# An RWKV-7 scan on one core: a substitution moved from VectorE to GpSimd, a multiply-add for the state, and another scheduler

## The chip, the cores and the metric

The kernel runs on one core of a Trainium2 chip. The metric is the device time of one execution in microseconds (us), the median of several runs of the same program. A profile is taken of one further execution; its span runs from the first to the last instruction.

Engines are named as in the profile: PE is TensorE (matrix products; PEld its weight loads), DVE is VectorE, ACT is ScalarE, POOL is GpSimd, SP is SyncE, which issues the DMAs here. Each engine works through a queue of its own in a fixed order; an instruction that waits for a semaphore holds up all behind it in that queue. SBUF is the on-chip memory, PSUM the banks that PE writes.

## The reference, cut to what matters

One encoder layer: x (1024 positions, 1024 channels) is normalised and multiplied by one wide matrix w_in; three mixers (an mLSTM, a long convolution by FFT, a bidirectional RWKV-7) work on parts of the product; their outputs are gated, merged, projected and added to x. The change is in the third mixer and in the scheduling of everything.

```python
def rwkv7_scan(r, w, k, v, kk, a, reverse):
    def step(state, inp):
        r_t, w_t, k_t, v_t, kk_t, a_t = inp
        sa = jnp.einsum('bhij,bhj->bhi', state, -kk_t)
        state = (state * w_t[:, :, None, :] + sa[..., None] * (kk_t * a_t)[:, :, None, :]
                 + v_t[..., None] * k_t[:, :, None, :])
        return state, jnp.einsum('bhij,bhj->bhi', state, r_t)
...
    y_fwd = rwkv7_scan(r_h, dec_h[:, :, 0], k_dir[:, :, 0], v_h, kk, a_h[:, :, 0], reverse=False)
    y_bwd = rwkv7_scan(r_h, dec_h[:, :, 1], k_dir[:, :, 1], v_h, kk, a_h[:, :, 1], reverse=True)
```

There are 16 heads of 64 channels, two directions and 1024 positions.

## The kernel before

**Chunks.** The scan works on pairs of heads (8 pairs) and chunks of 64 positions (16 chunks, `CL = 64`): 8 x 16 = 128 steps, each for two heads and both directions (d = 0 forward, d = 1 backward) at once. Inside a chunk the delta rule is a triangular system. Its inverse, the table `tt`, is computed ahead of the scan for eight chunks, both directions and both heads together, which I call a substitution: `tphase(cx, g)`, g = 0 for steps 0 to 7 and g = 1 for steps 8 to 15 of a pair, 16 substitutions in all.

**A substitution** (`tphase`, L1597): block products on PE (tile pq), copied by ACT to `quad` and `q21`; a transpose on DVE into `Ab`; a loop of 31 rounds l, each a multiply into `tm` of 31-l by l//2+1 elements per partition and an add into `Tb`, through the helper `self.tt` (L476, DVE); two more transposes on DVE (t1, t2); two rounds of small products on PE (tile pwx) with copies by ACT (W, tt). Each round needs the one before it.

**A step of the scan** (`scan`, L1740, one turn of the loop over m): U = products of G and SV on PE (tile pch); copied by DVE to `us`; SA = products of tt and us; copied into SV by DVE (first head) and ACT (second head); SN = products of B and SV; the state S1 = (SN + S0) x pc on DVE, two operations (pc is the decay of the chunk); S1 copied into the next step's SV, one half by DVE, one by ACT. Then the next step's U can start. The outputs of a step, products [G, SV] and [ar, sn], are issued inside the next step (`outputs`, `late`). `in_turn` (L391) issues a group of products one behind the other, with the lines L395 (first) and L398 (the rest).

**Other work of a pair**: `prep` (decays and scaled keys, on ACT and DVE; two-operand DVE work on tiles s, P, a, tmp, ar, bk; its small tile `s` is cleared by a POOL memset), `setup` (G, B and SV of the next two steps: products pgr and ptv), `load`, `bonus`, `post`.

**Fillers.** All products with w_in and later the branch projections are jobs (`gemm`, L343: 512-column products into tile pg, three for each weight: L351 to L353). Ahead of the scan they fill the other mixers; inside it `weave` (L72) lets a step yield four times and takes a share of the jobs that are left at each (`fill`). A weight tile is loaded by SP (`wraw`, 3 buffers), rounded by ACT (`wh`) and its remainder is made by POOL (`wl<-wraw,wh`, L334, 4 buffers).

**What sets the order.** The program is written with a tile framework: a list scheduler orders each engine's queue from the traced program, by priority; `high_priority(n)` moves instructions ahead by n, `issue_after` keeps one behind another on an engine. `put(gen, steps...)` in `rwkv` says at which yields of a pair (64 of them, 4 per step) a generator of other work is advanced.

Of the kernel before, what the change touches and what calls it, by code (L numbers as in the profile page):

```python
# [11 lines left out]
F32 = mybir.dt.float32  # L12
F32R = mybir.dt.float32r
AF = mybir.ActivationFunctionType
# [9 lines left out]
TP, PP, PW, RA = 400, 0, 3, 2  # L24
NP, ND = 3, 2
SA, SB = 100, 16
TAIL = (21, 22, 23)
CDEC = math.exp(-0.5)
MUL, ADD, SUB, MAX, MIN = ALU.mult, ALU.add, ALU.subtract, ALU.max, ALU.min
# [30 lines left out]
def ahead(tc, gen, by):  # L60

    while True:
        if by:
            with tc.high_priority(by):
                if next(gen, gen) is gen:
                    return
        elif next(gen, gen) is gen:
                return
        yield
# [43 lines left out]
class Row0:  # L113
# [133 lines left out]
    def first(self, w1t, bf):  # L247

        acc = self.ts(w1t[:, 0:1], 0.0, MUL)
        for i in range(1, 17):  # L250
            acc = self.tt(acc, w1t[:, i:i + 1], ADD)
        return self.act(acc, bf, 0)
# [33 lines left out]
class Trunk:  # L286
# [104 lines left out]
    def in_turn(self, calls, ins=None):  # L391

        for f in calls:
            if ins is None:
                ins = f()  # L395
                continue
            with self.tc.issue_after(ins.ins), self.tc.high_priority(10 ** 6):
                ins = f()  # L398
        return ins

    def banks(self, name):

# [944 lines left out]
    def rwkv(self, yc_out, pairs=range(8)):  # L1347
        nc, tc, A = self.nc, self.tc, self.A
        with ExitStack() as c2:
# [37 lines left out]

            pairs = list(pairs)
            n = len(pairs)
            cx = [dict(p=p, ar={}, al={}, bk={}, pc={}) for p in pairs]  # L1390
            run(self.load(cx[0]))
            for g in range(2):
# [8 lines left out]
            for i in range(n):  # L1401
                at = {}

                def put(gen, *steps):
                    for s in steps:
                        at.setdefault(s, []).append(gen)
                put(prep1, 0, 0, 1, 2, 3, 4, 4)
                put(self.bonus(cx[i]), 5, 6, 7)
                put(ahead(tc, self.tphase(cx[i], 1), TP), *range(6, 28, 2))
                if i + 1 < n:  # L1410
                    nx = cx[i + 1]
                    put(self.load(nx, cx[i - 1] if i else None), 8, 9, 10, 11)
                    put(ahead(tc, self.prep(nx, 0, 0), PP), 15, 16, 19, 33, 33)
                    put(ahead(tc, self.prep(nx, 0, 1), PP), 34, 35, 36, 37, 37)
                    put(ahead(tc, self.tphase(nx, 0), TP), *range(39, 62, 2))
                    prep1 = ahead(tc, chain(self.prep(nx, 1, 0), self.prep(nx, 1, 1)), PP)
                    put(prep1, 40, 42, 49)
                if i > 0:
                    put(self.post(cx[i - 1], yc_out, i + 1 == n), 5, 6, 7, 8, 11, 12, 13, 14)
                weave(self.scan(cx[i], cx[i + 1] if i + 1 < n else None), at, self.fill, max(0, self.left() - 6) / (64.0 * (n - i + 0.1)))  # L1420
# [176 lines left out]
    def tphase(self, cx, g):  # L1597

        nc, rp = self.nc, self.rp
        x2 = lambda n: self.ep.tile([128, 16, 32], F32, name=n, tag="x2", bufs=3)
        q, q21 = x2("quad"), self.ep.tile([128, 16, 32], F32, name="q21", tag="q21", bufs=1)
        pq = [x.rearrange("p (c t) -> p c t", t=CL) for x in self.banks("pq")]
# [25 lines left out]
        for l in range(31):  # L1630
            n, m = 31 - l, l // 2 + 1
            x = tm[:, 0:n * m].rearrange("p (a b) -> p a b", b=m)
            self.tt(x, Ab[:, l + 1:32, l].unsqueeze(2).broadcast_to([128, n, m]),
                    Tb[:, l, 0:m].unsqueeze(1).broadcast_to([128, n, m]))
            o = Tb[:, l + 1:32, 0:m]
            self.tt(o, o, x, ADD)
            if l % 5 == 4:
                yield
        tt = self.tt_t[g]
        t1 = x2("t1").rearrange("p a b -> p (a b)").rearrange("p (v s) -> p v s", s=16)  # L1640
        nc.vector.transpose(t1.rearrange("p v s -> p s v"), Tb.rearrange("p t s -> p s t"))
        t1 = t1.rearrange("p (g u) s -> p u s g", g=2)
        t2 = x2("t2")
        nc.vector.transpose(t2.rearrange("p u (s g) -> p u s g", g=2), t1)
# [95 lines left out]
    def scan(self, cx, nx):  # L1740
# [13 lines left out]
        for m in range(16):  # L1754
# [11 lines left out]
            if late:  # L1766
                late[0](ins)
            us = self.sm.tile([128, 2, CL], F32, name="us", tag="us", bufs=2)
            nc.vector.tensor_copy(us, U)  # L1769
            ins = self.in_turn(partial(nc.tensor.matmul, SA[hsl[h], d], tt[hsl[h], 8 * d + c, :], us[hsl[h], d],  # L1770
                                       start=True, stop=True) for d in range(2) for h in range(2))
            if late:
                late[1](ins)
            late = None
            nc.vector.tensor_copy(SV[0:64, 0, both], SA[0:64])
            nc.scalar.copy(SV[0:64, 1, both], SA[64:128])  # L1776
            yield
            next(ahead, None)
            yield
            self.in_turn(partial(nc.tensor.matmul, SN[hsl[h], d], B[:, j, d, hsl[h]], SV[:, h, at[d]],  # L1780
                                 start=True, stop=True) for d in range(2) for h in (1, 0))
            S1 = self.sm.tile([128, 2, 64], F32, name="sn", tag="sn", bufs=3)
            pc = cx["pc"][g][:, :, c:c + 1].broadcast_to([128, 2, 64])
            if m == 0:
                self.tt(S1, SN, pc)
            else:
                self.tt(S1, SN, S0, ADD)
                self.tt(S1, S1, pc)
            late = self.outputs(y, py, m, S0, ar, now)
            S0 = S1  # L1790
            if m < 15:
# [5 lines left out]
            if m < 15:  # L1797

                SV, at = now[2], now[4]
                nc.vector.tensor_copy(SV[0:64, 0, at], S1[0:64])  # L1800
                nc.scalar.copy(SV[0:64, 1, at], S1[64:128])  # L1801
            yield
            next(ahead, None)
            yield
# [111 lines left out]
```

## Time and profile before

| | |
|---|---|
| median of 3 runs | 2182.08 us (2180.28 to 2186.04) |
| profiled execution, its span | 2200.05 us, 2198.3 us |
| granted PE clock, mean | 0.956 |
| ahead of the scan, scan, behind it (first and last product of pch) | 929, 1059, 210 us |
| PE, DVE, ACT, POOL busy | 1994.0, 1634.6, 1103.2, 424.3 us |
| substitution loop (tm and Tb of L476), 16 x 62 operations on DVE | 145.4 + 144.2 us |
| POOL: wl split, 408 operations | 371.5 us |

A line of a group in the profile reads: line, engine, operation, output<-inputs by the program's names, shapes, count | busy us, mean ns of one | idle us of that engine just before them, and what ended it. A line of the timeline reads: start us, us, engine, line, operation, names, shapes, count, and in brackets the engine's idle time before it and who ended it.

### The profile page before, as it was taken

To read this page: it belongs to the slowest core of one execution; us is meant where nothing else is said; L and a number is where in the kernel's file an instruction comes from. 1 tells how busy PE (TensorE), PEld (TensorE's weight loads), DVE (VectorE), ACT (ScalarE), POOL (GpSimd) and SP (SyncE) were. 2 spreads that over 40 slices of the span, in tenths; PEclk is the share of its full clock that TensorE was granted. 3 is DMA by queue.
4 is the path that set the end of the run, shared out by engine and by line. 5 is a ranking of instruction groups with operands and counts; after the bars stand their busy time and mean duration, and the time that the engine had idled before them with its cause. 6 is when DMAs were issued, how large, how long until landed. Compare 5 with 4: busy or idle time off the path is not lost. (4 is left out here: it accounts for less than half of the span.)

```text
span 2198.3 us, 45984 instructions
## 1 busy us (share of the span) xinstructions
PE 1994.0 (91%) x17098; PEld 1509.2 (69%) x17098; DVE 1634.6 (74%) x4754; ACT 1103.2 (50%) x2558; POOL 424.3 (19%) x485
## 2 busy tenths in 40 slices
PE   6999899999989899899989999999898887897998
PEld 4666777787868677666766676666666665675786
DVE  4854999988447947788787888868887888764536
ACT  5557356454242115664665756667466564532221
POOL 2211311122222432311101111111114411010200
PEclk9999999999999999999998999999899998897999
DMA  8211222334465345321322333224143542445623
GB/s 255 70 67 59 78 77 90 112 101 127 143 200 172 119 138 163 124 68 61 130 79 93 117 106 102 92 81 136 52 155 118 187 144 63 159 143 175 196 89 129
DMA packets 169384, 262.19 MB, mean 119 GB/s; under 512 B 17863, under 2 KB 87335, under 8 KB 169160
## 3 DMA queue, kind: packets, MB, share of 16 engines
q1 hardware_dynamic: 169160, 259.25, 36.3%
q8 instruction: 135, 2.21, 0.4%
q14 instruction: 89, 0.73, 0.1%
HBM read 181.06 MB, written 78.12 MB: 118 GB/s over the span
## 5 line engine op out<-in xcount | busy, mean ns | idle before, releaser
L334 POOL TENSOR_TENSOR wl<-wraw,wh 128x256 fp32r<-128x256 f32 x408 | 371.5, 915 | 1488.6 <-ACT wh L333 1464.8
L351 PE MATMUL pg<-hh,wh 128*128 128x512 f32 x1440 | 601.5, 418 | 20.9 <-ACT wh L333 11.8
L352 PE MATMUL pg<-hh,wl 128*128 128x512 f32 x1440 | 594.3, 413 | 16.4 <-POOL wl L334 16.3
L353 PE MATMUL pg<-hl,wh 128*128 128x512 f32 x1440 | 592.4, 412 | 1.9 <-DVE hl L565 1.8
L351 PEld LDWEIGHTS pg<-hh,wh 128*128 128x128 f32 x1440 | 278.7, 194 | 88.9 <-ACT wh L333 15.1
L352 PEld LDWEIGHTS pg<-hh,wl 128*128 128x128 f32 x1440 | 279.3, 194 | 78.0 <-POOL wl L334 22.2
L353 PEld LDWEIGHTS pg<-hl,wh 128*128 128x128 f32 x1440 | 278.1, 193 | 62.0 <-DVE hl L565 2.8
L333 ACT CAST wh<-wraw 128x256 fp32r<-128x256 f32 x408 | 162.7, 404 | 220.6 <-PE pg L353 122.1
L476 DVE TENSOR_TENSOR tm<-Ab,Tb 128x126 f32<-128x126 f32 (+22 forms) x496 | 145.4, 293 | 4.4 <-DMA Tb<-in_tinit 2.7
L476 DVE TENSOR_TENSOR Tb<-Tb,tm 128x126 f32<-128x126 f32 (+22 forms) x496 | 144.2, 291 | 1.9
L473 DVE SCALAR_TENSOR_TENSOR st<-pg,hmu,st 128x511 f32<-128x511 f32 (+1 forms) x130 | 80.9, 636 | 27.9 <-ACT e L424 17.6
L476 DVE TENSOR_TENSOR G<-pgr,gmask 128x512 f32<-128x512 f32 x128 | 85.4, 679 | 17.0 <-PE pgr L398 17.0
L457 ACT ACTIVATE st<-pg 128x512 f32<-128x512 f32 x74 | 44.2, 597 | 99.9 <-PE pg L353 95.0
L1684 ACT COPY G<-ar 64x128 f32<-64x128 f32 x256 | 64.3, 295 | 48.4 <-DVE G L476 46.6
L473 DVE SCALAR_TENSOR_TENSOR st<-st,pg 128x512 f32<-128x512 f32 x80 | 54.3, 679 | 35.7 <-PE pg L353 12.7
L398 PE MATMUL pgr<-ar,bk 64*128 64x128 f32 x896 | 76.9, 287 | 0.0
L141 DVE SCALAR_TENSOR_TENSOR row<-row 64x1 f32<-64x1 f32 x393 | 72.7, 208 | 2.1
L1769 DVE COPY us<-pch 128x128 f32<-128x128 f32 x128 | 36.3, 283 | 45.8 <-PE pch L398 45.5
L395 PEld LDWEIGHTS pch<-SV,G 128*64 128x64 f32 x256 | 25.3, 139 | 65.5 <-ACT SV L1801 52.3
L395 PE MATMUL pch<-SV,G 128*64 128x64 f32 x256 | 43.2, 252 | 27.7 <-ACT SV L1801 26.2
L476 DVE TENSOR_TENSOR dw<-dw,dw 128x512 f32<-128x512 f32 x92 | 67.1, 760 | 0.9
L395 PEld LDWEIGHTS pch<-SV,B 128*64 128x64 f32 x256 | 25.3, 139 | 60.1 <-ACT SV L1776 50.1
(677 smaller groups left out, 4228.4 us busy)
## 6 DMA issues: line engine op xcount, KB each, us to landing
wraw<-in_w_in SPq DMA_DIRECT2D x340, 128.0 KB, 2.3
low<-lora SPq DMA_DIRECT2D x32, 512.0 KB, 4.1
sig<-st SPq DMA_DIRECT2D x48, 256.0 KB, 2.6
st<-sig SPq DMA_DIRECT2D x48, 256.0 KB, 3.5
wraw<-in_w_br SPq DMA_DIRECT2D x68, 128.0 KB, 2.8
adw<-in_ada_w SPq DMA_DIRECT2D x16, 512.0 KB, 7.1
x<-in_x SPq DMA_DIRECT2D x8, 512.0 KB, 6.1
hx<-st SPq DMA_DIRECT2D x16, 256.0 KB, 2.0
```

The lines of the kernel that those rows point to most:

```text
L141: self.ops.append(lambda: self.nc.vector.scalar_tensor_tensor(o, a, s, b, op0=op0, op1=op1))
L333: self.nc.scalar.copy(hi, raw)
L334: self.nc.gpsimd.tensor_tensor(lo, raw, hi.bitcast(F32), op=SUB)
L351: nc.tensor.matmul(p, wh, hh, start=(k == 0), stop=False)
L352: nc.tensor.matmul(p, wl, hh, start=False, stop=False)
L353: nc.tensor.matmul(p, wh, hl, start=False, stop=(k == n - 1))
L395: ins = f()
L398: ins = f()
L457: self.nc.scalar.activation(o, p, AF.Tanh, scale=0.5)
L473: return self.nc.vector.scalar_tensor_tensor(out, in0, s, in1, op0=op0, op1=op1)
L476: return self.nc.vector.tensor_tensor(out, a, b, op=op)
L1684: nc.scalar.copy(G[0:64, :, d, h, 0:64], cx["al"][g, d, b % 4][hsl[h]])
```

## The change

- The 62 operations of the substitution's loop go from DVE (`self.tt`) to POOL (`nc.gpsimd.tensor_tensor`).
- The first transpose behind the loop is kept behind the copy `us` of the step in which it is issued (`issue_after(self.mark.ins)`), and the yields at which a substitution is advanced change: the loop's pieces are issued at 7 yields in a row, the rest 10 or more yields later.
- The state: ACT prepares S0d = S1 x pc of the next chunk, and the next state is one multiply-add per direction on DVE, S1 = SN x pc + S0d, on 64 columns each.
- The copies of the scan's chain (us, SV) and the state's operations get the highest priority (`first`).
- The whole program is ordered by the framework's scheduler with a simulation of the timeline.

```diff
+    def first(self):
+        return self.tc.high_priority(10 ** 6)
...
+            self.mark = None
...
-                put(ahead(tc, self.tphase(cx[i], 1), TP), *range(6, 28, 2))
+                put(ahead(tc, self.tphase(cx[i], 1), TP), 6, *range(7, 14), 24, 26, 28)
...
-                    put(ahead(tc, self.tphase(nx, 0), TP), *range(39, 62, 2))
+                    put(ahead(tc, self.tphase(nx, 0), TP), 39, *range(40, 47), 57, 59, 61)
...
         for l in range(31):
             n, m = 31 - l, l // 2 + 1
             x = tm[:, 0:n * m].rearrange("p (a b) -> p a b", b=m)
-            self.tt(x, Ab[:, l + 1:32, l].unsqueeze(2).broadcast_to([128, n, m]),
-                    Tb[:, l, 0:m].unsqueeze(1).broadcast_to([128, n, m]))
+            nc.gpsimd.tensor_tensor(x, Ab[:, l + 1:32, l].unsqueeze(2).broadcast_to([128, n, m]),
+                                    Tb[:, l, 0:m].unsqueeze(1).broadcast_to([128, n, m]), op=MUL)
             o = Tb[:, l + 1:32, 0:m]
-            self.tt(o, o, x, ADD)
+            nc.gpsimd.tensor_tensor(o, o, x, op=ADD)
             if l % 5 == 4:
                 yield
+        yield
...
-        nc.vector.transpose(t1.rearrange("p v s -> p s v"), Tb.rearrange("p t s -> p s t"))
+        with tc.issue_after(self.mark.ins) if self.mark else ExitStack():
+            nc.vector.transpose(t1.rearrange("p v s -> p s v"), Tb.rearrange("p t s -> p s t"))
...
-            nc.vector.tensor_copy(us, U)
+            with self.first():
+                self.mark = nc.vector.tensor_copy(us, U)
...
-            nc.vector.tensor_copy(SV[0:64, 0, both], SA[0:64])
-            nc.scalar.copy(SV[0:64, 1, both], SA[64:128])
+            with self.first():
+                nc.vector.tensor_copy(SV[0:64, 0, both], SA[0:64])
+                nc.scalar.copy(SV[0:64, 1, both], SA[64:128])
...
-            pc = cx["pc"][g][:, :, c:c + 1].broadcast_to([128, 2, 64])
-            if m == 0:
-                self.tt(S1, SN, pc)
-            else:
-                self.tt(S1, SN, S0, ADD)
-                self.tt(S1, S1, pc)
+            pc = cx["pc"][g][:, :, c:c + 1]
+            with self.first():
+                if m == 0:
+                    self.tt(S1, SN, pc.broadcast_to([128, 2, 64]))
+                else:
+                    for d in range(2):
+                        self.stt(S1[:, d], SN[:, d], pc[:, d], S0d[:, d])
+            if m < 15:
+                S0d = rp.tile([128, 2, 64], F32, name="sd", tag="sd", bufs=2)
+                pc = cx["pc"][(m + 1) // 8][:, :, (m + 1) % 8:(m + 1) % 8 + 1]
+                for d in range(2):
+                    nc.scalar.activation(S0d[:, d], S1[:, d], AF.Copy, scale=pc[:, d])
...
-                nc.vector.tensor_copy(SV[0:64, 0, at], S1[0:64])
-                nc.scalar.copy(SV[0:64, 1, at], S1[64:128])
+                with self.first():
+                    nc.vector.tensor_copy(SV[0:64, 0, at], S1[0:64])
+                    nc.scalar.copy(SV[0:64, 1, at], S1[64:128])
...
-    with tile.TileContext(nc) as tc:
+    with tile.TileContext(nc, schedule_with_timeline_sim=True) as tc:
```

What the scheduler makes of it is seen in three places. A row is one instruction, or several alike (x3): line, operation, output<-inputs, size of the output. Line numbers of the changed kernel are 4 to 18 higher.

PE, in the middle of the third pair, before: one step of the scan from its U (pch<-SV,G) through the products of the outputs (pch<-G,SV) to SA (pch<-us,tt), with products with w_in (pg) between.

```order
L395 MATMUL pch<-SV,G 64x64
L398 MATMUL pch<-SV,G 64x64 x3
L398 MATMUL pch<-G,SV 64x64 x4
L1704 MATMUL ptv<-cmat,vp 128x128 x2
L351 MATMUL pg<-hh_134,wh 128x512
L352 MATMUL pg<-hh_134,wl 128x512
L353 MATMUL pg<-hl_135,wh 128x512
L351 MATMUL pg<-hh_136,wh 128x512
L352 MATMUL pg<-hh_136,wl 128x512
L353 MATMUL pg<-hl_137,wh 128x512
L395 MATMUL pch<-us,tt_8478 64x64
L398 MATMUL pch<-us,tt_8478 64x64 x3
```

The same place now, from U to SN (pch<-SV,B):

```order
L395 MATMUL pch<-SV,G 64x64
L398 MATMUL pch<-SV,G 64x64 x3
L398 MATMUL pch<-G,SV 64x64 x4
L395 MATMUL pch<-us,tt_8478 64x64
L398 MATMUL pch<-us,tt_8478 64x64 x3
L398 MATMUL pch<-ar,sn 64x64 x4
L1557 MATMUL plw<-low,w2h 128x512
L1557 MATMUL plw<-low,w2l 128x512
L1712 MATMUL ptv<-cmat,vp 128x128 x2
L395 MATMUL pch<-SV,B 64x64
L398 MATMUL pch<-SV,B 64x64 x3
```

No product with w_in is left here; in the third and the seventh pair there are 0 and 2 of them in 16 steps, and the scan has 1335 of them in place of 1700.

DVE, the end of a substitution in that pair, before: loop operations (tm, Tb) stand between the scan's copies (us, SV) and the preparation's work.

```order
L476 TENSOR_TENSOR tm<-Ab,Tb 128x56
L1769 COPY us<-pch 128x128
L476 TENSOR_TENSOR Tb<-Tb,tm 128x4x14
L476 TENSOR_TENSOR bk<-tmp,s 128x4x64
L476 TENSOR_TENSOR tm<-Ab,Tb 128x45
```

Now, from a step's us through the next step's:

```order
L1778 COPY us<-pch 128x128
L1649 STREAM_TRANSPOSE t_13585<-Tb 128x16x32
L480 TENSOR_TENSOR G<-pgr,gmask 128x4x128
L480 TENSOR_TENSOR a<-k,a 128x512
L480 TENSOR_TENSOR G<-pgr,gmask 128x4x128
L1652 STREAM_TRANSPOSE t_13587<-t_13585 128x512
L1785 COPY SV<-pch 64x2x64
```

The loop has left DVE, and the transpose that waits for its end on POOL stands between us and the copy SV<-pch of the same step.

POOL, early in the scan, before: splits of weights (wl), with memsets between.

```order
L334 TENSOR_TENSOR wl<-wraw,wh 128x256 x2
L1555 MEMSET s 128x8 x2
L1699 MEMSET SV 64x512
L334 TENSOR_TENSOR wl<-wraw,wh 128x256 x15
L1555 MEMSET s 128x8
```

Now, between the first and the second pair, where the loop of one substitution ends and the next begins:

```order
L334 TENSOR_TENSOR wl<-wraw,wh 128x256
L1638 TENSOR_TENSOR tm<-Ab,Tb 128x16
L1641 TENSOR_TENSOR Tb<-Tb,tm 128x16
L334 TENSOR_TENSOR wl<-wraw,wh 128x256 x17
L1638 TENSOR_TENSOR tm<-Ab,Tb 128x31
L1641 TENSOR_TENSOR Tb<-Tb,tm 128x31
L1638 TENSOR_TENSOR tm<-Ab,Tb 128x30
```

The splits stand in groups ahead of a loop or among its last rounds, and 62 operations of the loop or more follow each other without one.

More of the change, by code (lines that the diff above doesn't have):

```diff
@@ L1597, in tphase @@
     def tphase(self, cx, g):
-        nc, rp = self.nc, self.rp
+        nc, tc, rp = self.nc, self.tc, self.rp
         x2 = lambda n: self.ep.tile([128, 16, 32], F32, name=n, tag="x2", bufs=3)
```

## The prediction, on record before the changed kernel was run

> **What bounds the kernel now.** I read the busy line of the page, then busy time by stage, then the timeline of one scan step and of one substitution, then groups of instructions for prices.
>
> ```profile
> span 2198.3 us, 45984 instructions
> PE 1994.0 (91%) x17098; PEld 1509.2 (69%) x17098; DVE 1634.6 (74%) x4754; ACT 1103.2 (50%) x2558; POOL 424.3 (19%) x485
> 0.00:929.00 929.00, 850.10 (x4178) 658.33 (x4178) 684.38 (x2119) 428.85 (x913) 235.13 (x247) 0.97 0.38 123
> 929.00:1987.80 1058.80, 958.15 (x12167) 704.90 (x12166) 845.07 (x2464) 624.04 (x1552) 169.66 (x215) 0.95 0.34 109
> 1987.80:2198.30 210.50, 185.75 (x756) 145.94 (x756) 105.15 (x172) 50.29 (x94) 19.48 (x23) 0.92 0.47 154
> 0.00:50.00 50.00, 31.17 (x226) 21.66 (x230) 21.78 (x46) 26.58 (x46) 11.40 (x13) 0.93 0.96 271
> 550.00:600.00 50.00, 50.00 (x218) 40.58 (x217) 25.51 (x39) 14.02 (x32) 13.14 (x16) 1.00 0.37 129
> ```
>
> The columns of a stage are its length, then busy time (and count) of PE, PEld, DVE, ACT and POOL. PE is the bound, and time is lost where it idles: 79 us before the scan (19 of them at the start), 101 us in the scan, 25 us behind it, 204 in all. The change takes no work off PE, so it gains what it removes of these 204 us and loses what it adds. The last row gives the price of a 512-column matmul when they follow each other: 50.00 / 218 = 0.229 us. I call those of the weight products GEMMs.
>
> In the order before, 1700 GEMMs stand between the scan's first and last step, 0 to 33 in each of its 128 steps. In the changed order there are 1335, in clusters. I count in halves of a pair (8 steps, one substitution each, for tables used 8 steps later). Four halves have 288, 336, 261 and 213 GEMMs. Eleven halves with a substitution, which I call light, have 0 to 123, and those at their start: 67, 0, 0, 0, 0, 27, 123, 0, 2, 0, 18. The last half has no substitution and none. 365 GEMMs have moved ahead of the scan; 364 stand behind it in both orders.
>
> **How long a light half takes** is the main term. Two chains run in it: the scan's steps and the substitution. Here is one step of before with no GEMM in it:
>
> ```profile
> 1860.68 0.37 PE L395 MATMUL pch<-SV,G 128*64 128x64 f32 x1 [1.16 <-ACT SV L1801]
> ...
> 1861.43 0.29 DVE L1769 COPY us<-pch 128x128 f32<-128x128 f32 x1 [0.17 <-PE pch L398]
> ...
> 1861.77 0.36 PE L395 MATMUL pch<-us,tt 64*64 64x64 f32 x1
> ...
> 1863.20 0.37 PE L395 MATMUL pch<-SV,B 128*64 128x64 f32 x1 [0.31 <-ACT SV L1776]
> ...
> 1864.02 0.29 DVE L476 TENSOR_TENSOR sn<-pch,sn 128x128 f32<-128x128 f32 x1 [0.46 <-PE pch L398]
> ...
> 1864.35 0.29 DVE L476 TENSOR_TENSOR sn<-sn,pc 128x128 f32<-128x128 f32 x1
> ...
> 1865.02 0.37 PE L395 MATMUL pch<-SV,G 128*64 128x64 f32 x1 [1.12 <-ACT SV L1801]
> ```
>
> The next step begins 1865.02 - 1860.68 = 4.34 us later. And one whole substitution of before, from its block products (pq) to the products behind it (pwx):
>
> ```profile
> 1825.79 1.73 PE L398 MATMUL pq<-ar,bk 64*32 64x32 f32 x107
> 1830.21 1.99 DVE L1625 STREAM_TRANSPOSE Ab<-quad 128x1024 f32<-128x1024 f32 x1
> 1832.95 0.21 DVE L476 TENSOR_TENSOR tm<-Ab,Tb 128x31 f32<-128x31 f32 x1 [0.51 <-DMA Tb<-in_tinit]
> 1866.68 0.15 DVE L476 TENSOR_TENSOR Tb<-Tb,tm 128x16 f32<-128x16 f32 x1
> 1867.43 1.10 DVE L1641 STREAM_TRANSPOSE t<-Tb 128x512 f32<-128x512 f32 x1
> 1868.67 1.83 PE L398 MATMUL pwx<-t,q 32*32 32x32 f32 x61
> 1873.11 1.83 PE L398 MATMUL pwx<-t,W 32*32 32x32 f32 x61
> ```
>
> pq starts 7.2 us ahead of the first multiply; the loop itself takes 1866.83 - 1832.95 = 33.9 us on DVE, between its other work; 8.1 us later pwx is done, of which I take 2 us off for GEMMs that stood between. In the changed order the next pq stands 1.6 steps behind pwx, 1.6 x 4.34 = 7.0 us. So a light half takes 7.2 + T + 6.0 + 7.0 = 20.2 us + T, where T is the loop's time, if that is more than 8 x 4.34 = 34.7 us with nothing else in it. It is, unless T is under 14.5: PE reaches pwx in the sixth or seventh step and stands there, and DVE stands at its transpose, behind which the copy SV<-pch of that step is queued, so the scan stands too. What hid this in before is GEMMs.
>
> **T on GpSimd.** The loop is 31 multiplies and 31 adds over 5712 elements per partition in all (from its bounds: twice the sum of (31-l)(l//2+1)).
>
> ```profile
> L334 POOL TENSOR_TENSOR wl<-wraw,wh x408: 715/742/10347, 34.0 to 2091.0; 128x256 fp32r<-128x256 f32 x136
> L1108 POOL TENSOR_TENSOR hl<-st,hh x16: 1267/1316/2142, 1666.0 to 1729.1; 128x512 fp32r<-128x512 f32 x16
> 198.87 0.95 POOL L671 MEMSET rm<- 64x1024 f32 x1
> 199.88 0.11 POOL L672 MEMSET rm<- 64x8 f32 x1
> L476 DVE TENSOR_TENSOR tm<-Ab,Tb x496: 151/255/1658, 869.5 to 1937.0; 128x126 f32<-128x126 f32 x15, 128x56 f32<-128x56 f32 x12, 128x110 f32<-128x110 f32 x12, 128x78 f32<-128x78 f32 x10
> ```
>
> The medians at 256 and 512 elements give (1316 - 742) / 256 = 2.24 ns an element and 742 - 573 = 169 ns an instruction: 62 x 0.169 + 5712 x 0.00224 = 23.3 us. Each of the 62 now waits for POOL's instruction before it; the memsets, where the second waits so, stand 0.06 us apart: 3.7 us. That is 27 us with POOL undisturbed. POOL is disturbed:
>
> ```profile
> 757.60 17.06 POOL L334 TENSOR_TENSOR wl<-wraw,wh 128x256 fp32r<-128x256 f32 x2 [4.18 <-ACT wh L333]
> ...
> 758.86 3.69 DVE L473 SCALAR_TENSOR_TENSOR dw<-dw,dw 128x512 f32<-128x512 f32 x6
> L1800 DVE COPY SV<-sn x120: 171/209/1305, 935.5 to 1982.2; 64x128 f32<-64x128 f32 x120
> L1769 DVE COPY us<-pch x128: 236/285/294, 929.5 to 1983.3; 128x128 f32<-128x128 f32 x128
> L1564 DVE TENSOR_TENSOR_SCAN s<-smask,s 128x520 f32<-128x520 f32 x32 | 39.7, 1240 | 10.8 <-ACT s L1561 9.8 <-issue 1.0
> L476 DVE TENSOR_TENSOR ar<-r,P 128x256 f32<-128x256 f32 x64 | 29.8, 465 | 0.0
> L476 DVE TENSOR_TENSOR bk<-a,s 128x256 f32<-128x256 f32 x64 | 29.0, 456 | 0.1
> L473 DVE SCALAR_TENSOR_TENSOR ar<-kk,P 128x256 f32<-128x256 f32 x64 | 28.2, 440 | 5.4 <-PE pch L398 5.4
> L476 DVE TENSOR_TENSOR bk<-tmp,s 128x256 f32<-128x256 f32 x64 | 27.2, 430 | 3.9 <-ACT s L1567 3.6
> L476 DVE TENSOR_TENSOR a<-k,a 128x512 f32<-128x512 f32 x32 | 23.3, 727 | 3.7 <-ACT mm L1572 3.6
> L473 DVE SCALAR_TENSOR_TENSOR tmp<-a,kk 128x512 f32<-128x512 f32 x32 | 22.6, 707 | 2.8 <-ACT a L1560 2.8
> ```
>
> Two POOL splits that take 0.74 us each stretched over 17.06 us while DVE ran elementwise work on two SBUF operands without a break. In the other direction the SBUF copy SV<-sn, 0.209 us, took up to 1.305, while the copy from PSUM never passed 0.294: an operand in PSUM is out of it. So each two-SBUF instruction of DVE inside the loop's time adds about its length to T. The seven groups shown sum to 199.8 us, 12.5 per half; at 38 of a half's 58 us, 8 us fall inside. With the smaller ones that the changed DVE order has between Ab and the transpose (products for the bonus and the previous pair's output) I take 11: T = 38 us, between 27 (none) and 46 (all that a half has, some 19). A light half is then 58 us, between 47 and 66.
>
> The Trainium skill (GPSIMD Engine Reference, section 4.1) advises against this move: elementwise work of two inputs is about 2x slower on GpSimd than on VectorE. By the rows above it is 27 us against 62 x 0.256 = 15.9, 1.7x; with 2.0x the loop would be 31.8 us undisturbed and, with the 11 us, 43 us.
>
> **The sum**, against the span of 2198.3 us.
> Scan: the four halves with GEMMs are bound by PE. PE works 958 - 1700 x 0.229 = 569 us in the scan beside GEMMs, 35.6 per half; 4 x 35.6 + 1098 x 0.229 = 394 us. Their substitutions lie beside the GEMMs, and so does POOL's weight split while the four buffers of wl are ahead. Of the 237 other GEMMs about 100 stand ahead of pq and lengthen their half: 23 us. The last half takes 36. Eleven light halves of 58.2: 640. Sum 1093, +34 on 1058.8.
> Ahead of the scan: 365 x 0.229 = 84 us more on PE, less what of the 79 us idle the earlier GEMMs fill: nothing to all 60 past the start; I take half, +53, between +24 and +84.
> Behind the scan: the same products, 0.
> Other queues: SP issues the same DMAs, those of the moved GEMMs (weights in, results out) earlier; DMA is 0.38 busy ahead of the scan, 0. POOL's memsets of s, for which the next preparation on ACT waits, now stand in groups behind a whole loop, up to T late; they stand a half ahead of need, 0, and the price if that is gone is in the last rival but one.
> State: two operations on the path (0.29 each above, in a row) become two on 64 columns:
>
> ```profile
> L476 DVE TENSOR_TENSOR y<-y,pch 128x64 f32<-128x64 f32 x128 | 24.8, 209 | 7.4 <-PE pch L398 7.1
> L1735 ACT COPY y<-pch 128x64 f32<-128x64 f32 x128 | 21.0, 214 | 36.3 <-PE pch L398 35.5
> ```
>
> 2 x 0.209 for 2 x 0.29: 0.16 us a step, 20 us over 128 steps if it were all on the path. In light halves T ends later, in the others PE works on, so I take 0 (20 at most). The decayed state is 240 ACT operations at 0.214 = 51 us on an engine that is idle 435 of the scan's 1059 us; they stand behind or beside the scan's copies, 0, at worst their 0.43 us on 36 steps, 15. The copies put first save at most the one DVE instruction that they waited behind; hidden in the same way, 0. DVE loses 62 x 0.256 x 16 = 254 us of work, which matters only through T.
> Together +87: a span of 2285. The profiled execution took 2200.05 against a median of 2182.08, so I scale by 0.992: 2267 us, 3.9% slower. PE would then idle 291 us in place of 204.
>
> **Rivals.**
> Faster: POOL is hardly held up, T = 27, light halves 47.2 us: 453 + 519 = 972 in the scan, -87 + 53 = -34, about 2147 us. For it: in the changed order DVE has no loop of its own, so POOL's gaps of 0.06 us and DVE's idle time may not meet; against it: the 17.06 us above. It decides at T = 30.1, where the sum is 0.
> Short rows: the loop's operands are strided or repeated, in rows of 1 to 16 elements, and no row of the trace has such on POOL. If they cost 0.08 us an operation more than the contiguous ones, T = 43: 453 + 11 x 63.2 = 1148, +142, 2321 us. (The 2x of the Trainium skill, GPSIMD Engine Reference, section 4.1, would lead here.)
> Bursts: DVE holds POOL out for all of a half's work and the GEMM clusters wait for wl behind a run of the loop: T = 46, with +84 ahead of the scan, +206, 2385 us. For it: PE waited for wl in before too, with far less on POOL.
>
> ```profile
> PEld pg L352 <- POOL wl L334: 24.9, 18, 7.0
> ```
>
> The change does not do what it says: the loop is not what ends a light half and the moved GEMMs fill idle time only, so that the loss in the scan and the gain elsewhere cancel: 2182.
>
> **Chances.** Forecast (2200 to 2300) 0.50; short rows 0.14; bursts 0.09; cancel 0.05; faster 0.22. A difference of 0.3% is about what the runs can tell from none. Slower by more: 0.73; same 0.05; faster 0.22. The range 2140 to 2365 leaves out most of the bursts and the part of the faster case in which the 60 us of idle time ahead of the scan are all filled too; the forecast alone spans 2200 to 2300.
>
> **What would show it.** The first step of the scan starts at 960 to 1010 us. Runs of 62 POOL operations last 32 to 45 us each, with means of 0.5 us or more. PE idles before pwx for DVE's transpose, and DVE before its transpose for POOL, about 10 to 20 us in each light half; light halves are 50 to 65 us long, the four others 90 to 115 at a PE busy share near 10 tenths. If the runs on POOL take 27 us or less, or the scan begins before 950, the forecast is wrong on the side of faster; if SV<-sn or the scan's ACT copies show long waits in halves where T is over, a step itself is longer than 4.34 us and it is wrong on the other.

## The result: 17% slower, and the profile after

The changed kernel takes 2553.07 us (median of 4 runs, 2542.3 to 2554.53), before in the same series 2184.06: a ratio of 1.1665, 95% interval 1.1604 to 1.1727. The forecast had the sign, and with 2267 us (2140 to 2365) far too small a size.

The page of the changed kernel (span, busy line, granted clock in 40 slices):

```profile
span 2540.1 us, 46353 instructions
PE 2108.9 (83%) x17098; PEld 1654.5 (65%) x17098; DVE 1458.2 (57%) x3762; ACT 1181.1 (46%) x2796; POOL 839.9 (33%) x1477
PEclk9999799999999998889689766797699665666999
```

Busy time by stage, with the columns of before (length; PE, PEld, DVE, ACT, POOL; granted clock):

```profile
0.00:1018.00 1018.00, 927.11 (x4538) 732.66 (x4539) 701.35 (x2085) 450.18 (x966) 278.08 (x341) 0.96 0.38 121
1018.00:2329.00 1311.00, 996.81 (x11778) 774.58 (x11778) 649.08 (x1499) 681.22 (x1735) 541.12 (x1113) 0.76 0.25 82
2329.00:2540.10 211.10, 184.95 (x790) 147.21 (x786) 107.72 (x178) 49.70 (x95) 20.69 (x23) 0.93 0.46 153
```

The span is 342 us longer: 90 ahead of the scan (its first copy `us` at 1019.4, before at 929.5), 255 in it, -3 behind. No engine is the bound in the scan: PE works 997 of 1311 us although 365 weight products have left the scan, and part of that is the lower clock (0.76 against 0.95), which stretches each record. DVE has lost 196 us of work there and waits. Four halves of the scan, cut at every eighth `us`: an even one (steps 0 to 7 of the third pair), the odd one behind it, one with weight products, and the last, which has no substitution:

```profile
1399.50:1480.50 81.00, 53.72 (x715) 40.33 (x716) 46.34 (x102) 52.10 (x130) 29.34 (x65) 0.65 0.27 86
1480.50:1537.10 56.60, 39.07 (x634) 31.30 (x634) 32.41 (x86) 28.18 (x74) 28.43 (x64) 0.62 0.07 25
1618.30:1729.80 111.50, 94.86 (x892) 73.92 (x893) 46.23 (x104) 52.30 (x130) 61.30 (x106) 0.89 0.31 103
2296.00:2332.50 36.50, 25.88 (x356) 20.64 (x356) 14.22 (x57) 12.97 (x42) 0.00 (x0) 0.66 0.01 1
```

Numbered from 0, the four halves with weight products (1, 3, 7, 9) take 110, 114, 112 and 108 us. The same halves of before took 65, 65, 65 and 61, so they are 188 us longer; they hold 1101 weight products in place of 399, and 702 x 0.229 = 161 us. The eleven light halves together lost 1017 weight products, 233 us of PE work, and became 69 us longer: the odd ones, with next to no products left (0, 0 and 2 in halves 5, 11 and 13), take 56.6, 56.1 and 56.2 us, the eight even ones 74 to 101, in the mean 83.

What ends an even half, in the chain of waits from the end of its loop (1455.60) to its end (start, us, what):

```profile
1456.17 0.27 DVE t L1649
...
1459.76 0.62 ACT tt L1663
1460.39 0.62 ACT tt L1664
...
1462.29 0.26 ACT SV L1786
...
1462.57 0.69 ACT s L1562
...
1463.28 0.58 ACT W L1662
...
1464.47 0.63 ACT s L1566
...
1465.36 0.30 ACT SV L1819
...
1472.80 1.24 PE plw L1557 x2
1474.06 4.42 DMA low<-lora
...
1478.61 1.19 PE plw L1557 x2
```

The loop is over, and the half goes on for 25 us. The scan's copies SV (L1786, L1819) stand in ACT's queue behind copies of `tt` and `W` and the next pair's preparation (`s`), then PE stands at `plw` until the DMA of `low` has landed. The step in which the loop ends takes 13.8 us, the two behind it 12.7 and 11.9.

The loop itself and the new operations (busy us, mean ns, then the idle time before them):

```profile
L1638 POOL TENSOR_TENSOR tm<-Ab,Tb 128x126 f32<-128x126 f32 (+22 forms) x496 | 223.1, 450 | 230.0 <-DVE Ab L1630 180.4 <-DVE SV L1818 14.7
L1641 POOL TENSOR_TENSOR Tb<-Tb,tm 128x126 f32<-128x126 f32 (+22 forms) x496 | 224.8, 453 | 37.3 <-POOL tm L1638 0.2
L1649 DVE STREAM_TRANSPOSE t<-Tb 128x512 f32<-128x512 f32 x16 | 17.3, 1082 | 10.5 <-POOL Tb L1641 10.5
L477 DVE SCALAR_TENSOR_TENSOR sn<-pch,pc,sd 128x64 f32<-128x64 f32 x240 | 56.6, 277 | 143.9 <-PE pch L398 130.7 <-ACT hh L1111 4.9 <-ACT B L1702 4.5
L1805 ACT ACTIVATE sd<-sn,pc 128x64 f32<-128x64 f32 x240 | 81.5, 346 | 82.9 <-DVE sn L477 79.6
```

From its first multiply to its last add the loop takes 31.7 to 38.8 us in the light halves, 33.6 in the mean. DVE's transpose waits for it only 10.5 us in all.

The loop is on the path all the same. The page's chain of work that ended last, by engine and by line:

```profile
PE 30%; POOL 16%; DVE 11%; DMA 10%; issue 9%; ACT 7%; SPq 1%; DVEq 0%; POOLq 0%; ACTq 0%
POOL Tb L1641 7%; POOL tm L1638 7%; PE pg L352 6%; PE pg L351 6%; PE pg L353 6%; PE pout L1263 3%; DVE dw L480 2%; DMA st<-sig 2%; POOL wl L334 1%; PE pch L395 1%; DMA wraw<-in_w_in 1%; PE pch L398 1%; DVE st L477 1%; PE pG L957 1%; DVE G L480 1%
```

In ten of the eleven light halves the loop's two operations hold 16 to 29 us of that chain. In the odd half above, DVE waits for the last add, and the scan's copies SV come behind the transpose (and, on ACT, behind copies of `tt`):

```profile
1522.25 1.05 DVE L1649 STREAM_TRANSPOSE t<-Tb 128x512 f32<-128x512 f32 x1 [2.22 <-POOL Tb L1641]
...
1525.00 0.24 DVE L1785 COPY SV<-pch 64x128 f32<-64x128 f32 x1
...
1527.63 0.26 ACT L1786 COPY SV<-pch 64x128 f32<-64x128 f32 x1
```

But the loop doesn't end a half: 15 to 33 us of each light half follow its last add.

### The profile page after: what moved, and what is told of

It is laid out like the page before. It is cut to its first block, busy times and chain, and to the rows that moved or that the text cites. A ratio compares the mean times of both kernels' runs of the same rounds, so it can differ in the third digit from the quotient of the medians.

```text
span 2540.1 us, 46353 instructions
## 1 busy us (share of the span) xinstructions
PE 2108.9 (83%) x17098; PEld 1654.5 (65%) x17098; DVE 1458.2 (57%) x3762; ACT 1181.1 (46%) x2796; POOL 839.9 (33%) x1477
## 4 chain that ended last, share of the span: by engine, by line
PE 30%; POOL 16%; DVE 11%; DMA 10%; issue 9%; ACT 7%; SPq 1%; DVEq 0%; POOLq 0%; ACTq 0%
POOL Tb L1641 7%; POOL tm L1638 7%; PE pg L352 6%; PE pg L351 6%; PE pg L353 6%; PE pout L1263 3%; DVE dw L480 2%; DMA st<-sig 2%; POOL wl L334 1%; PE pch L395 1%; DMA wraw<-in_w_in 1%; PE pch L398 1%; DVE st L477 1%; PE pG L957 1%; DVE G L480 1%
## 5 line engine op out<-in xcount | busy, mean ns | idle before, releaser
L334 POOL TENSOR_TENSOR wl<-wraw,wh 128x256 fp32r<-128x256 f32 x408 | 347.5, 856 | 1035.6 <-ACT wh L333 949.0
L351 PE MATMUL pg<-hh,wh 128*128 128x512 f32 x1440 | 575.9, 407 | 30.5 <-DVE st L477 24.4
L352 PE MATMUL pg<-hh,wl 128*128 128x512 f32 x1440 | 577.8, 403 | 8.2 <-POOL wl L334 7.7
L353 PE MATMUL pg<-hl,wh 128*128 128x512 f32 x1440 | 573.5, 401 | 1.2 <-POOL hl L1112 1.2
L1638 POOL TENSOR_TENSOR tm<-Ab,Tb 128x126 f32<-128x126 f32 (+22 forms) x496 | 223.1, 450 | 230.0 <-DVE Ab L1630 180.4
L1641 POOL TENSOR_TENSOR Tb<-Tb,tm 128x126 f32<-128x126 f32 (+22 forms) x496 | 224.8, 453 | 37.3 <-POOL tm L1638 0.2
L477 DVE SCALAR_TENSOR_TENSOR sn<-pch,pc,sd 128x64 f32<-128x64 f32 x240 | 56.6, 277 | 143.9 <-PE pch L398 130.7
L1805 ACT ACTIVATE sd<-sn,pc 128x64 f32<-128x64 f32 x240 | 81.5, 346 | 82.9 <-DVE sn L477 79.6
L395 PE MATMUL pch<-SV,B 128*64 128x64 f32 x256 | 52.1, 297 | 60.8 <-ACT SV L1786 60.6
L398 PE MATMUL pgr<-ar,bk 64*128 64x128 f32 x896 | 96.8, 338 | 0.0
```

The source lines that it names most:

```text
L334: self.nc.gpsimd.tensor_tensor(lo, raw, hi.bitcast(F32), op=SUB)
L351: nc.tensor.matmul(p, wh, hh, start=(k == 0), stop=False)
L352: nc.tensor.matmul(p, wl, hh, start=False, stop=False)
L353: nc.tensor.matmul(p, wh, hl, start=False, stop=(k == n - 1))
L477: return self.nc.vector.scalar_tensor_tensor(out, in0, s, in1, op0=op0, op1=op1)
L1638: nc.gpsimd.tensor_tensor(x, Ab[:, l + 1:32, l].unsqueeze(2).broadcast_to([128, n, m]), Tb[:, l, 0:m].unsqueeze(1).broadcast_to([128, n, m ...
```

## Experiments

All start from before or from the changed kernel; all ratios are against before. "First" is the first `us`, "even", "odd" and "last" are mean lengths of the halves (eight, seven, one), worked out from the starts of `us`.

| run | median us | ratio (95%) | first | scan | even, odd, last |
|---|---|---|---|---|---|
| before | 2180 to 2192 | 1 | 930 | 1058 | 70, 65, 38 |
| changed | 2553 | 1.1665 (1.160-1.173) | 1019 | 1313 | 83, 88, 37 |
| e1 simulation only | 2545 | 1.1655 (1.162-1.169) | 1023 | 1316 | 83, 88, 36 |
| e2 changed, no simulation | 2337 | 1.071 (1.067-1.074) | 911 | 1211 | 80, 74, 49 |
| e3 loop on GpSimd only | 2327 | 1.064 (1.061-1.068) | 907 | 1198 | 88, 64, 48 |
| e4 state only | 2218 | 1.015 (1.010-1.019) | 916 | 1077 | 74, 64, 41 |
| e12 copies first only | 2225 | 1.018 (1.015-1.021) | 917 | 1097 | 72, 70, 38 |
| e5 simulation, gated at U | 2588 | 1.181 (1.178-1.185) | 982 | 1386 | 99, 76, 67 |
| e6 changed, gated at U | 2523 | 1.151 (1.147-1.155) | 979 | 1331 | 98, 69, 65 |
| e9 simulation, spread | 2400 | 1.097 (1.094-1.100) | 980 | 1202 | 81, 72, 54 |
| e14 changed, spread | 2377 | 1.085 (1.080-1.090) | 979 | 1183 | 85, 64, 54 |
| e7 no simulation, moved | 2331 | 1.064 (1.060-1.069) | 978 | 1136 | 77, 68, 39 |
| e8 e3 + splits on VectorE | 2208 | 1.009 (1.005-1.012) | 921 | 1074 | 78, 58, 46 |
| e15 e3 + some splits | 2237 | 1.023 (1.017-1.029) | 919 | 1103 | 80, 60, 43 |
| e11 e8 + priority | 2260 | 1.033 (1.029-1.037) | 937 | 1118 | 81, 61, 39 |
| e10 e14 + splits on VectorE | 2347 | 1.074 (1.070-1.077) | 980 | 1156 | 83, 63, 54 |
| e13 e9 + copies first | 2400 | 1.096 (1.091-1.101) | 983 | 1197 | 80, 72, 57 |
| e16 e9, PE pinned | 2449 | 1.120 (1.114-1.126) | 978 | 1262 | 87, 72, 56 |
| e17 e9, three engines pinned | 2416 | 1.105 (1.100-1.110) | 970 | 1235 | 85, 72, 56 |
| e18 changed, low apart | 2550 | 1.167 (1.161-1.173) | 1016 | 1326 | 83, 90, 37 |

### One part at a time

e1, the simulated timeline alone:

```diff
-    with tile.TileContext(nc) as tc:
+    with tile.TileContext(nc, schedule_with_timeline_sim=True) as tc:
```

> Before, with the simulated timeline as the only edit; the loop stays on VectorE, the state and copies as before. Theory O (the order: weight products leave 11 of 16 halves, and the work of the next preparation stands between the scan's steps): the order has 1288 weight products in the scan, in clusters as in the changed kernel (20, 288, 0, 336, 0, 0, 0, 264, 24, 251, 85, 0, 0, 2, 18, 0 by halves), so most of the +370 us must come: 2430 to 2560 us, light halves of 70 to 85 us, a granted clock below 0.8 in the scan. Theory G (the loop on GpSimd sets the length of a light half): with the loop on VectorE only the products moved ahead of the scan count, 2200 to 2300 us. Theory S (the decayed state on ScalarE): 2180 to 2230.

e2 takes this one line out of the changed kernel.

> The changed kernel without the simulated timeline. The order then has 1686 weight products in the scan, 85 to 119 in every half, 2558 ahead of it and 460 behind. Theory O: within 2% of before, 2140 to 2230 us, because weight products cover the loop and the copies again; granted clock in the scan 0.9 or more. Theory G: each of 15 halves waits for the loop, 2300 or more. Theory S: 2250 to 2350, since the 240 operations of the decayed state (346 ns each) stand in the scan's chain in any order.

e3 is before with the loop on GpSimd, its yields and the transpose behind `us` (these hunks of the change).

> Before, with the loop on GpSimd, its yields and the transpose behind us, and nothing else. 1686 weight products in the scan, 78 to 148 in each half. Theory O: -30 to +20 us, 2150 to 2200 (VectorE loses 254 us of work that weight products hid in part). Theory G: +100 or more, 2280 or more. Theory S has no part here: 2180.

e4 is before with the hunks of the state, e12 with `first()` around the scan's copies and state.

> Before, with the multiply-add for the state and the decayed state on ScalarE, and nothing else. 1700 weight products in the scan, as before. Theories O and G: 2160 to 2195 us (0.16 us a step saved at most 20, 83 us of ScalarE work hidden). Theory S: 2230 or more.

> Before with the scan's copies and state operations at the highest priority and nothing else; 1700 weight products in the scan. All theories: -10 to +10 us, 2170 to 2200; by halves the last four have 117, 74, 125 and 9 weight products.

e1 settles which part is enough: the one line gives all of the loss, with the loop still on VectorE. Its scan has the same length and halves as the changed kernel's:

```profile
1023.00:2338.70 1315.70, 1006.85 (x11753) 778.23 (x11753) 835.64 (x2432) 608.09 (x1490) 125.98 (x179) 0.74 0.25 80
```

On top of it the rest of the change costs nothing that can be told from the spread (2553 against 2545 us, ratios 1.1665 and 1.1655). That doesn't mean that the rest is free: without the simulation (e2) the three other parts take 2337 us together, which fits theories G and S and not O; the loop on GpSimd alone costs 139 us (e3), the state 30, the copies put first 36, against about 0 expected for the last two. The parts do not add up. The misses of e4 and e12 are small (1.5 and 1.8%) but clear of their intervals, and lie in the scan (+19 and +39 us by the profiles); what in it, was not followed up. For the state the price is seen above: 2 x 277 ns in place of 2 x 0.29 us, so nothing is saved, and ScalarE gets 76 to 82 us more.

### Where the weight products stand

e5 and e6 keep each share of weight products on PE behind the U products of the step that issues it:

```diff
+    def gated(self, n):
+        with self.tc.issue_after(self.gate.ins):
+            self.fill(n)
...
             ins = self.in_turn(partial(nc.tensor.matmul, U[hsl[h], d], ...
+            self.gate = ins
```

> Before with the simulated timeline, and each share of weight products kept on PE behind the U products of the step in which the program issues it. By halves the order has 116, 102 to 108 in thirteen, 101 to 108 in the rest (1723 in the scan, 2536 ahead, 445 behind); all else is ordered by the simulation. Theory C (halves without weight products are what costs): 2150 to 2240 us, granted clock in the scan above 0.9. Theory P (the simulation puts the preparation's work between the scan's copies, with weight products or without): 2350 us or more.

> The changed kernel with the same rule for the weight products (1719 in the scan, 102 to 116 in each half). Theory C: about what the changed kernel without the simulation took, 2300 to 2360 us, since the loop on GpSimd still holds up the splits wl. Theory P: 2420 us or more.

By the numbers this is theory P, but e5 got slower than e1, which neither had foreseen. The order shows why these two cannot tell them apart: 12 to 18 weight products now stood in one place, between U and tt, where the scan waits 1.2 us and they take 2.7 or more. e9 therefore sets the gate anew behind each of the scan's three groups; e14 does it in the changed kernel.

```diff
             ins = self.in_turn(... tt[hsl[h], 8 * d + c, :], us[hsl[h], d], ...
+            self.gate = ins
...
-            self.in_turn(partial(nc.tensor.matmul, SN[hsl[h], d], B...
+            self.gate = self.in_turn(partial(nc.tensor.matmul, SN[hsl[h], d], B...
```

> Before with the simulated timeline, and each share of weight products kept on PE behind the last scan products issued ahead of it (U, tt or B), so that they stand as in before in two places of a step, 6 behind the tt products and 6 to 12 behind the B products; in the run gated behind U alone 12 to 18 stood between U and tt, 2.7 us or more in a wait of 1.2 us. By halves 102 to 108 (1710 in the scan). Theory C (the loss of the simulated order is where it puts the weight products: out of most halves, in heaps in others): halves as in before, 60 to 75 us, 2180 to 2270 in all. Theory P (it is the order of the preparation and set-up among the scan's steps): 80 us or more a half, 2400 or more.

> The changed kernel with spread weight products (1704 in the scan, 102 to 108 a half), the splits wl on GpSimd as in the changed kernel. With the splits on VectorE it took 2347. If splits behind a loop hold up the weight products as in the run with only the loop on GpSimd (2327 against 2208): 2440 to 2480, so that the changed kernel with its heaps (2553) loses less than 115 us by them. If not: 2340 to 2380.

e9 landed at theory P's mark, but 146 us below e1, and e14 came out 176 us below the changed kernel, in its lower case. So heaps and empty halves are 41% of the loss in the one and 48% in the other: both theories have a part. These shares include whatever the granted clock gave back, which is 0.74 in e1's scan and 0.92 in e9's. e7 comes from the other side: before's own scheduler, with the weight products issued early.

```diff
+            quota = [q / 32.0 for q in [3,48,0,56,0,0,0,44,4,42,14,0,0,0,3,0]]
+            self.fill(69)
...
-        owed += per
+        owed += per[min(i // 32, 1)]
```

> Before with its own scheduler, but the program issues the weight products early: 69 shares ahead of the scan, the rest in the first halves. By halves the order has 104, 202, 153, 183, 159, 84, 111, 49, 115, 76, 89, 49, 0, 2, 18, 0 (1394 in the scan, 2946 ahead). Theory C: the last four halves are empty and take 70 to 85, 55 to 65, 70 to 80 and 36 us, as in the simulated order; 2230 to 2330 in all, clock below 0.8 there. Theory P: without the simulation an empty half is 7 + 34 + 13 = 54 us as in the prediction; the last four take 200 us or less, 2150 to 2220 in all.

It took 2331 us, the upper end of theory C; theory P's 2220 is far off. Its last four halves, with 0, 2, 18 and 0 weight products:

```profile
1874.10:1950.40 76.30, 52.80 (x698) 40.01 (x696) 53.42 (x153) 45.12 (x109) 0.34 (x3) 0.60 0.24 80
1950.40:2011.30 60.90, 41.82 (x658) 33.35 (x660) 45.09 (x159) 23.88 (x62) 0.63 (x2) 0.65 0.18 62
2011.30:2075.90 64.60, 48.34 (x684) 38.27 (x682) 37.70 (x124) 30.88 (x85) 0.73 (x1) 0.61 0.24 82
2075.90:2114.60 38.70, 28.70 (x372) 23.18 (x371) 16.41 (x59) 8.60 (x30) 0.00 (x0) 0.63 0.01 1
```

and the same halves of before, with 117, 56, 106 and 50:

```profile
1749.60:1821.80 72.20, 64.38 (x823) 47.41 (x821) 60.70 (x166) 48.30 (x118) 10.34 (x15) 1.00 0.48 152
1821.80:1884.10 62.30, 50.93 (x704) 37.84 (x702) 51.53 (x166) 27.73 (x70) 5.08 (x7) 0.78 0.25 81
1884.10:1948.70 64.60, 59.16 (x770) 43.30 (x769) 46.99 (x137) 33.04 (x92) 6.34 (x8) 0.95 0.52 173
1948.70:1987.50 38.80, 35.13 (x433) 25.59 (x431) 20.23 (x64) 11.48 (x36) 3.68 (x5) 0.91 0.25 77
```

This is the pair of views to learn from. 240.5 us with 20 weight products, 237.9 with 329 of them, whatever PE's busy share says (64.38 of 72.20). Taken out, up to some 110 in a half leave nothing behind that is shorter, and they cost time where they go: halves 1 to 4 of e7 hold 262 more than before's, 60 us of PE work, and are 61 us longer; ahead of the scan 306 more, 70 us of work, put its start off by 49 us.

Why an empty half is no shorter has two readings, and e7 doesn't separate them. One is that the half is as long as its chain of scan, substitution and preparation, so that the products lay in waits. The other is the clock, 0.60 to 0.65 in the empty halves against 0.78 to 1.00: the scan's own products, 1258 and 1266 records of `pch`, kept PE busy for 85.6 us in e7's four halves and 66.5 in before's. How long an empty half would be at the full clock, no run shows.

### The splits behind the loop

e8 is e3 with the splits of the scan on VectorE; e15 does so only at the yields beside a loop; e11 is e8 with the shares of weight products raised by a priority of 200; e10 is e14 with e8's edit.

```diff
-        self.nc.gpsimd.tensor_tensor(lo, raw, hi.bitcast(F32), op=SUB)
+        eng = self.nc.vector if self.mark else self.nc.gpsimd
+        eng.tensor_tensor(lo, raw, hi.bitcast(F32), op=SUB)
```

> The run with only the loop on GpSimd, and inside the scan the splits wl made by VectorE, so that none of them stands behind a loop on GpSimd. Theory W (that run lost its 139 us because weight products wait for wl, 137 us of PE idle): PE's wait for wl falls below 20 us and the time to 2170 to 2230. Rival (the loop itself, 34 to 40 us long, is waited for by the scan): 2300 or more.

> The loop on GpSimd in before's own scheduler, and the splits wl on VectorE only at the yields beside a loop (6 to 23 and 39 to 56 of 64), else on GpSimd; nothing else is changed. With all splits of the scan on VectorE: 2208. If VectorE's 190 splits in the scan are what ate the gain of the lighter VectorE: 2165 to 2195. If splits issued beside a loop still queue behind it, or the halves' length isn't VectorE's: 2200 to 2240.

> The loop on GpSimd with the splits on VectorE (2208 us, 0.9% slower than before), and the shares of weight products issued in the scan raised by a priority of 200. There 459 products stood behind the last tt product and the last four halves took 96, 64, 81 and 46 us, with the first twelve 2.5 us shorter than in before. Now 364 stand behind, 2636 ahead, and the last four halves have 126, 91, 171 and 46. If the late products are what cost the gain: last four halves about 250 us, 2150 to 2185 in all. If a half with the loop on GpSimd is no shorter: 2190 to 2220.

> The changed kernel (loop on GpSimd, multiply-add, copies first, simulated timeline) with the same two rules: weight products spread behind the scan's products, 102 to 108 a half, and the splits wl made by VectorE in the scan. Theory C together with W: 2208 us of the run with loop on GpSimd and splits on VectorE, plus 30 for the state, 2200 to 2290. Theory P: 2400 or more.

What PE waited for splits, in e3, in e8, and in the changed kernel (us in all, times, longest):

```profile
PE pg L352 <- POOL wl L334: 137.4, 30, 14.7
```

```profile
PE pg L355 <- POOL wl L337: 25.1, 11, 12.3
```

```profile
PE pg L352 <- POOL wl L334: 10.2, 10, 2.6
```

e8 took back 119 of e3's 139 us, so the queue on GpSimd is shown as the cause there. In the changed kernel it hardly counts: few weight products are left beside a loop; with them spread again (e14 against e10) it is worth 30 us. With the loop on GpSimd and the splits on VectorE the odd halves are shorter (58 us in e8, 65 in before) and the even ones longer (78, 70). e15 and e11, which were to keep the first without the second, came out above e8 (e11 above both of its cases), and no run beat before. e10, e9's rule and e8's together, fell between its two cases.

### What is left of the simulated order

e9 still loses 196 us by its profile, 51 ahead of the scan and 144 in it:

```profile
850.00:980.40 130.40, 50.55 (x452) 36.19 (x450) 88.03 (x171) 43.32 (x71) 2.49 (x6) 0.61 0.27 91
980.40:2182.00 1201.60, 998.05 (x12216) 753.23 (x12216) 871.27 (x2471) 641.89 (x1568) 166.83 (x216) 0.92 0.30 96
```

Ahead of the scan the other mixers end late: the last of their pG products starts at 752 us, before at 679. The simulated order runs weight products earlier there (2323 by 800 us in the changed kernel, 2252 in before); in e9 PE has none left for the last 130 us and works 50.55. The 71 products more are 16 of the 73 us by which pG ends later; the rest was not followed up. In the scan, PE's waits in e9 and in before:

```profile
PE pch L399 <- DVE us L1774: 52.2, 83, 3.5
PE pch L399 <- ACT SV L1807: 51.4, 39, 4.9
PE phs L1436 <- ACT hsp L1433: 31.1, 7, 16.8
PE plw L1556 <- DMA low<-lora: 25.9, 12, 4.0
```

```profile
PE pch L395 <- ACT SV L1801: 26.2, 25, 5.4
...
PE pch L395 <- DVE us L1769: 11.7, 20, 2.6
PE plw L1552 <- DMA low<-lora: 8.9, 10, 1.6
PE phs L1432 <- ACT hsp L1429: 7.3, 8, 2.2
```

These four are 107 us more than in before (160.6 - 54.1), all places where scan and preparation meet. e13 puts `first()` around the scan's copies in e9; e16 also keeps the products of preparation, set-up and substitution on PE behind the gate, e17 those on VectorE and ScalarE too; e18 gives `low` a buffer apart from `hsp` in the changed kernel.

```diff
         for g in at.pop(i, ()):
-            next(g, None)
+            with held():
+                next(g, None)
```

```diff
-        low = self.ep.tile([128, 2, 512], F32R, name="low", tag="low", bufs=1)
+        low = self.ep.tile([128, 2, 512], F32R, name="low", tag="lowp", bufs=1)
```

> The simulated order with spread weight products (2400 us, halves of 76 us in the mean against 68 in before) and in addition the scan's copies and state operations at the highest priority. If the 8 us a half are copies queued behind preparation work: halves of 68 to 71, 2270 to 2320. If priority doesn't matter to the simulation or the 8 us lie in other waits (products of the preparation on PE, the set-up itself): 2380 to 2420.

> Simulated order, spread weight products (2400 us), and the products of preparation, set-up and substitution (plw, phs, pgr, ptv, pq, pwx) on PE no earlier in its queue than the program issues them. If the 8 us a half are such products standing too early in PE's queue, where the scan's products wait behind them: halves of 68 to 71 us, 2270 to 2320. If they lie in the queues of VectorE and ScalarE: 2380 to 2420.

> The same on PE, VectorE and ScalarE: the order inside the scan is then the program's to within a step. If the loss in the scan is the simulation's order of preparation and set-up in any of the three queues: halves of 67 to 70 us, 2250 to 2300 (2182 + 51 ahead of the scan + up to 20 for the 98 weight products that trail behind it). If the loss stays, above 2380, the order of these queues is not its cause.

> The changed kernel with a buffer of its own for low, which it shares with hsp, so that a load of low no longer waits for the head sums that read hsp. If the waits for low add to the halves: PE's wait for it falls from 35.0 us to below 15, and the time by 15 to 35 us, 2518 to 2538. If the load waits for the products that read low before it, or other work ends as late: 2540 to 2565.

None of them gave anything back; e17 is a little slower than e9, and e16 is slower than both of its cases. In e18 PE's wait for `low` fell from 35.0 to 22.4 us, not to below 15, and the time stayed:

```profile
PE plw L1557 <- DMA low<-lora: 35.0, 20, 3.8
```

```profile
PE plw L1557 <- DMA low<-lora: 22.4, 12, 4.4
```

Other work ended as late. Which order would take e9's 144 us in the scan away is open; a pin only forbids an earlier place in a queue, not a later one. That the preparation's work in the scan's queues is the whole of it is what the waits suggest, and it isn't shown.

## Why the prediction was wrong

- **A light half is 20.2 us + T.** This is the step that failed, +170 of the 255 us that the span was missed by. It put 640 + 23 us on eleven halves; they took 833. T was sized well (38; measured 33.6). The fixed part was not. Cut as in the prediction, and in the mean of the light halves, pq to the loop takes 8.2 us (forecast 7.2), the loop's end to that of pwx 15.2 (6.0), and from there to the next pq 12.9 (7.0). The time after the loop is the failure: I had taken it from a substitution of before, and the steps in it at 4.34 us, from a step in which no preparation stood; in the even half above the two steps behind the loop take 12.7 and 11.9 us. The sign named for this, long waits of the scan's ACT copies after T is over, is what the chain shows. That an odd half without products (56.1 to 56.6 us) comes near 20.2 + 33 = 53 is luck: from its pq to the next, which is what the formula adds up, it is 63 us.
- **The cover of weight products.** I called PE the bound (91% busy) and added weight products to 35.6 us per half. The four halves that have them took 443 us in place of 394: PE, which was to be busy throughout, stood idle for 55 us in them. And e7's three halves with a substitution and next to no products, at 61 to 76 us, are as long as before's with theirs.
- **Ahead of the scan +53.** It was +90: I let the moved products, 365 x 0.229 = 84 us, fill 30 us of idle time; they filled none.
- **PE idles before pwx, and DVE before its transpose, 10 to 20 us in each light half.** Right in kind and far too large: DVE's transpose waited for the loop 10.5 us in sixteen. The loop is a leg of the path and not its end. e1, with the loop on VectorE, has the same halves and takes 36 us in the mean from first multiply to last add in the light ones; so the loop's engine is not the cause, and whether a shorter loop would shorten a half, no run shows. I had given 0.05 to the case that the loop is not what ends a light half, and a loss of nothing.
- **State and copies at 0.** Alone they cost 30 and 36 us; the bounds given were 20 gained and 15 lost. The multiply-add takes 277 ns and the decayed state 346, where the nearest rows said 209 and 214.
- **Bursts, a rival at 0.09.** Its mechanism exists (137 us in e3), but not in this order (10.2 us).
- **Short rows.** 450 ns a GpSimd operation is 1.7 times the 269 to 274 on VectorE in e1, as worked out, and 1.5 times the 291 to 293 in before. The 2x of the Trainium skill (GPSIMD Engine Reference, section 4.1) is more than this case shows.
- **Behind the scan 0**: -3, right. The granted clock was not considered; it fell to 0.76 in the scan. What that cost is not separated from the rest. An estimate: of the chain that ended last, PE's pieces are 100 us in the eleven light halves, and at the full clock in place of 0.62 to 0.79 they would be some 30 us shorter.

## What to carry to other kernels

A busy engine is not yet the bound: ask how long a stage would be without its filler, from a stretch that has none or by a run without it, before pricing filler that moves, and look at the granted clock of that stretch. When a change sets a scheduler's mode together with edits by hand, run the mode alone first; here it was all of the loss, and the edits' own costs (a split queued behind the loop, 137 us of waits) were hidden under it. Take the length of a chain's step from a stretch with the set-up and preparation that it will meet, not from the cleanest one.

## What the hardware showed beside

In the scan the granted clock goes with how busy PE is: 0.60 to 0.65 in halves of e7 with PE 69 to 75% busy, 0.91 to 1.00 in halves of before where it was busy 89 to 92% of the time. The Trainium skill (TensorE: Matmul & The Clock Gate, part 1) has two states, half and full rate, set by how busy PE has just been. The trace agrees: in the changed kernel the granted clock is 0.50 from 1430.5 to 1484.5 us and 1.00 from 1301 to 1406, and a mean of 0.62 is a mix of both.

The lower clock lengthens the records: a scan product's record is 229 to 242 ns in the mean in fourteen halves of before, 266 to 300 in the light halves after, and PE's busy sum is 115 us larger with the same products. Where PE's products are on the path, that is time; the last half, all steps of the scan, still took 36.5 us at 0.66 with no weight products and 38.8 at 0.91 with 50. A busy sum that rises with no more work is a sign of the clock and not of a fuller PE.
